# Feed-forward by seven block products: input sums kept in DRAM, other buffer homes, another order in one chunk

## The chip, the cores and the metric

One Trainium2 chip; the kernel runs on one of its cores. The metric is the device time of one execution in microseconds (us). Engines: PE (TensorE) does the matrix products, DVE (VectorE), ACT (ScalarE) and POOL (GpSimd) work elementwise, SP (SyncE) and ACT start the DMA transfers.

## What is computed

One decoder layer on x of 2048 tokens by 1024 channels, in float32:

```python
h = _rmsnorm(x, norm_mix_pre[i])
proj = jnp.einsum("btd,de->bte", h, w_in[i])
...                       # gated short convolution beside a Mamba-2 scan
mix = jnp.einsum("bte,ed->btd", jnp.concatenate([y_a, y_s], axis=-1), w_out[i])
x = x + _rmsnorm(mix, norm_mix_post[i])
h = _rmsnorm(x, norm_mlp_pre[i])
f = jnp.square(jax.nn.relu(jnp.einsum("btd,df->btf", h, w_up[i])))
f = jnp.einsum("btf,fd->btd", f, w_down[i])
x = x + _rmsnorm(f, norm_mlp_post[i])
```

w_up is 1024 x 4096, w_down 4096 x 1024.

## The kernel before

**Mixer.** Four blocks (b) of 512 tokens run one after the other: projections (L154 to L156), convolutions, the scan, the output projection (`out_half`, L166 to L168). What is left of block b at its end (the output projection of group 1, `post_norm`, `mlp_input`) goes into the list `pend` and is emitted by `drain(n)` calls between the stages of block b+1; `mlp_input` writes the normed hidden state, transposed, to `h2_d[b]` in DRAM. After the last block `drain(2)` emits the two halves of its last output projection before the feed-forward part; the other eight entries come by `drain(1)` after each of the first up steps.

**Every product in three.** A float32 operand is split into hi and lo parts (`split`: ACT casts, L609; DVE subtracts, L610), and each product is three matmuls: hi·hi, hi·lo, lo·hi.

**Feed-forward, up.** Two groups g of 1024 tokens. Both matrices are cut 2 x 2 and multiplied with seven block products in place of eight (Winograd's form of Strassen), in the order ORDER = 0, 1, 5, 6, 4, 2, 3. For each group `hidden_blocks` loads 16 tiles of `h2_d` (ring `xt`, 4 tiles), ACT multiplies each by its gain (L657), POOL forms the four sums t1 to t4 per k (L635, L636, L638, L642, ring `us`), and the 28 blocks (7 products x 4 k) are split into 56 tiles that stay for the whole group, k by k: all seven blocks of k = 0, then of k = 1, and so on. Where block i lives is `HOMES[i]`: rings of the mixer used a second time, among them `yh` and `yl`, which hold the inputs of the last output projection. Then for p = 0 to 15: `up_weights(p)` loads four tiles, makes four sums on POOL (L619 to L625) and seven splits into the rings `wh`, `wl` (8 tiles each); `up` does 7 products of 12 matmuls (L690 to L692), 84 per p; DVE adds them up (L697), ACT applies relu and square and its queue stores the result to `f_d`.

**Down weights.** After up(g, p), where p % 2 == g, `down_weights(p)` loads four tiles of w_down, makes four sums, seven splits through the same rings `wh` and `wl`, and stores the 14 parts to `dn_d[p]` from the ACT queue (L682): 18 transfers of 256 KB.

**Down.** For each group eight chunks of two p. `f_load` loads 4 tiles per p (L731, ring `raw`, 6 tiles), makes sums and splits them into the homes; `down_load` loads 14 parts of `dn_d` per p into the homes (L721, L722). A chunk is 28 accumulations (7 products x 4 token tiles) of 6 matmuls (L746 to L748) each. In the first chunk ACT copies them to `acc` tiles (L751), later DVE adds to those (L753). Chunks run product by product; the last chunk of each group is sorted by token tile (`todo.sort`), so that after the seven products of a token tile `combine` and `finish` (norm, gain, residual, store; L759 to L777) can begin.

**Order.** The calls above give instructions; the build lays out each engine's order from what is ready, and places and releases the tiles, so calls of different stages interleave: the first POOL sum of `hidden_blocks(0)` (L635) runs at 1092.4 us, some 400 us before the first up product. A ring tile (`big(tag)`) can be taken again once everything that reads it is done. All tiles here are 128 x 512 float32, 256 KB.

Of the kernel before, what the change touches and what calls it, by code (L numbers as in the profile page):

```python
# [8 lines left out]
F32 = mybir.dt.float32  # L9
F32R = mybir.dt.float32r  # L10
AF = mybir.ActivationFunctionType
ALU = mybir.AluOpType
# [3 lines left out]
P = 128  # L16
T = 2048
D = 1024
KT = D // P
TB = 512  # L20
NB = T // TB
# [4 lines left out]
FF = 4096  # L26
# [3 lines left out]
C_GPRE, C_GMLP, C_GOUT, C_CA, C_CS, C_CB, C_DSK = 0, 8, 16, 32, 56, 104, 116  # L30
# [2 lines left out]
C_ALL = 1536  # L33
BUFS = {
# [4 lines left out]
    "mix": 8, "epx": 2, "eph": 3, "gain": 2,  # L39
    "us": 4, "uc": 8, "acc": 28, "fx": 2,  # L40
}


# [1 line left out]
def hybrid_layer(ctx: ExitStack, tc: tile.TileContext, x, xT, w_in, w_dt, w_out, w_up, w_down,  # L45
# [8 lines left out]
    def big(tag, dt=F32):  # L54
        return sb.tile([P, 512], dt, tag=tag, name=tag, bufs=BUFS.get(tag, 1))
# [403 lines left out]
    def mlp_input(m, tok):  # L459
        for i in range(2):  # L460
            pt = bank()
            for k in range(4):
# [4 lines left out]
            S.dma_start(h2_d[tok // TT][:, i * 4:(i + 1) * 4, t * P:(t + 1) * P],  # L467
                        ht.rearrange("p (k t) -> p k t", k=4))

    gpost = [big("gain") for _ in range(2)]  # L470
    for i in range(2):
        SY.dma_start(gpost[i], rows[0:1, i * 512:(i + 1) * 512].broadcast_to([P, 512]))
# [2 lines left out]
    def drain(n):  # L475
        for _ in range(min(n, len(pend))):
            pend.pop(0)()
# [18 lines left out]
    for b in range(NB):  # L496
# [78 lines left out]
        for h in range(2):  # L575
# [1 line left out]
        ea = [lambda mix=mix, b=b, t=t: post_norm(mix[t], b * TT + t) for t in range(TT)]  # L577
        eb = [lambda mix=mix, b=b, t=t: mlp_input(mix[t], b * TT + t) for t in range(TT)]
        pend += [ea[0], ea[1], eb[0], ea[2], eb[1], ea[3], eb[2], eb[3]]
    drain(2)  # L580

    PB = 2 * TB
    NP = FF // P // 2
    NG = T // PB
    B7 = range(7)
    f_d = [[[dram.tile([P, TB], F32, name=f"f{g}_{f}_{q}") for q in range(2)]
            for f in range(FF // P)] for g in range(NG)]
    dn_d = [[[dram.tile([P, 512], F32, name=f"dn{p}_{i}_{s}") for s in range(2)]  # L590
             for i in B7] for p in range(NP)]

    gmlp = [big("gain") for _ in range(2)]
    for i in range(2):
        S.dma_start(gmlp[i], rows[1:2, i * 512:(i + 1) * 512].broadcast_to([P, 512]))


    HOMES = (("hh",) * 8, ("hl",) * 8, ("xs",) * 6 + ("conv",) * 2, ("xdt",) * 4 + ("z",) * 4,
             ("row",) * 4 + ("m",) * 4, ("yh",) * 8, ("yl",) * 8)

    def home(i, n):
        return HOMES[i][2 * n], HOMES[i][2 * n + 1]

    def ring(i):
        return "wh", "wl"

    def split(v, tags):
        hi, lo = (big(t, F32R) for t in tags)
        S.copy(hi, v)  # L609
        V.tensor_sub(lo, v, hi.bitcast(F32))  # L610
        return hi, lo


    def left(a11, a12, a21, a22, tags, eng):
        out = [None] * 7
        out[0] = split(a11, tags(0))
        out[1] = split(a12, tags(1))
        s1, s2, s3, s4 = (big("us") for _ in range(4))
        eng.tensor_tensor(s1, a21, a22, op=ALU.add)  # L619
        eng.tensor_tensor(s2, s1, a11, op=ALU.subtract)  # L620
        out[5] = split(s2, tags(5))
        eng.tensor_tensor(s3, a11, a21, op=ALU.subtract)
        out[6] = split(s3, tags(6))
        out[4] = split(s1, tags(4))
        eng.tensor_tensor(s4, a12, s2, op=ALU.subtract)  # L625
        out[2] = split(s4, tags(2))
        out[3] = split(a22, tags(3))
        return out

    def right(b11, b12, b21, b22, tags, eng):  # L630
        out = [None] * 7
        out[0] = split(b11, tags(0))
        out[1] = split(b21, tags(1))
        t1, t2, t3, t4 = (big("us") for _ in range(4))
        eng.tensor_tensor(t1, b12, b11, op=ALU.subtract)  # L635
        eng.tensor_tensor(t2, b22, t1, op=ALU.subtract)  # L636
        out[5] = split(t2, tags(5))
        eng.tensor_tensor(t3, b22, b12, op=ALU.subtract)  # L638
        out[6] = split(t3, tags(6))
        out[4] = split(t1, tags(4))  # L640
        out[2] = split(b22, tags(2))
        eng.tensor_tensor(t4, b21, t2, op=ALU.subtract)  # L642
        out[3] = split(t4, tags(3))
        return out

    ORDER = (0, 1, 5, 6, 4, 2, 3)

    def hidden_blocks(g):
        cols7 = [[None] * 4 for _ in B7]
        for k in range(4):  # L650
            raw = {}
            for j in range(2):
                gk = cp[:, C_GMLP + 4 * j + k:C_GMLP + 4 * j + k + 1]
                for q in range(2):
                    raw[j, q] = big("xt")
                    SY.dma_start(raw[j, q], h2_d[2 * g + q][:, 4 * j + k, :])
                    S.activation(raw[j, q], raw[j, q], AF.Copy, scale=gk)  # L657
            blocks = right(raw[0, 0], raw[0, 1], raw[1, 0], raw[1, 1], lambda i: home(i, k), G)
            for i in B7:
                cols7[i][k] = blocks[i]  # L660
        return cols7

    def up_weights(p):
        raw = {}
# [7 lines left out]
    def down_weights(p):  # L672
        raw = {}
        for j in range(2):
            for k in range(2):
                raw[j, k] = big("raw")
                SY.dma_start(raw[j, k].rearrange("p (a b) -> p a b", a=1),
                             w_down[2 * p + j][:, k:k + 1, :])
        blocks = right(raw[0, 0], raw[0, 1], raw[1, 0], raw[1, 1], ring, G)
        for i in ORDER:  # L680
            for s in range(2):
                S.dma_start(dn_d[p][i][s], blocks[i][s].bitcast(F32))  # L682

    def up(g, p, hb7, wb7):
        def product(i):
# [48 lines left out]
    def down(ps_, g, acc, last):  # L734
        first = ps_[0] == 0
        fb = [f_load(g, p, m) for m, p in enumerate(ps_)]
        wb = [down_load(p, m) for m, p in enumerate(ps_)]
        todo = [(i, t) for i in ORDER for t in range(TT)]
        if last:
            todo.sort(key=lambda it: it[1])  # L740
        for n, (i, t) in enumerate(todo):
            ts = slice(t * P, (t + 1) * P)
            pt = bank(("ax", "mm")[n % 2])
            for m in range(len(ps_)):
                (fh, fl), (wh, wl) = fb[m][i], wb[m][i]
                PE.matmul(pt, lhsT=fh[:, ts], rhs=wh, start=(m == 0), stop=False)  # L746
                PE.matmul(pt, lhsT=fh[:, ts], rhs=wl, start=False, stop=False)  # L747
                PE.matmul(pt, lhsT=fl[:, ts], rhs=wh, start=False, stop=(m == len(ps_) - 1))  # L748
            if first:
                acc[i, t] = big("acc")  # L750
                S.copy(acc[i, t], pt)  # L751
            else:
                V.tensor_tensor(acc[i, t], acc[i, t], pt, op=ALU.add)  # L753
            if last and i == ORDER[-1]:
                combine(g, acc, t)
# [14 lines left out]
    def finish(m, tok):  # L770
        r = norm_scale(m, "fx")
        for i in range(2):
# [3 lines left out]
            V.scalar_tensor_tensor(m[i], m[i], r, xt, op0=ALU.mult, op1=ALU.add)  # L776
            S.dma_start(out[tok * P:(tok + 1) * P, i * 512:(i + 1) * 512], m[i])  # L777

    for g in range(NG):
        hb7 = hidden_blocks(g)  # L780
        for p in range(NP):
            wb7 = up_weights(p)
            up(g, p, hb7, wb7)
            drain(1)
            if p % 2 == g:
                down_weights(p)
    for g in range(NG):
        acc = {}
        for p in range(0, NP, 2):
# [42 lines left out]
```

## Time and profile before

| | us |
|---|---|
| three runs | 2862.94, 2860.70, 2855.56; median 2860.7 |
| profiled execution, its time | 2856.19 |
| its span, first to last instruction | 2854.5 |
| mean granted clock of PE in it | 0.980 |

How to read it: the page gives the busy time of each engine and 40 slices; a table of windows gives, for each stretch of time, each engine's busy time with its number of instructions in brackets, the granted PE clock, the share of the DMA engines and their GB/s. Matmuls are pipelined, so PE's busy time hides slow ones; the number of matmuls in a stretch tells more. A list of waits has, for each pair of waiter and releaser, the total in us, the number of times and the longest. A timeline row has start, duration, engine, line, operation, and in brackets the idle time before it and what ended that. A group row has the number of instructions, their busy time in us, and the mean in ns.

### The profile page before, as it was taken

Reading aid. Unit: us, or ns where it says so; the run is one execution under the profiler, and the core shown is the slowest. Engines: PE = TensorE matmul, PEld = TensorE weight load, DVE = VectorE, ACT = ScalarE, POOL = GpSimd, SP = SyncE. Lnnn points to the kernel's source line nnn. Section 1 sums busy time; section 2 is a strip of 40 time slices with the busy share of each in tenths; the row PEclk is TensorE's granted clock in tenths of the full one; section 3 lists DMA queues with packets and bytes.
Section 4 is the critical chain, followed back from the end, with each engine's and each line's share of the span. In section 5 each row is a group of like instructions: output and inputs, shape, how many; then the busy total and the mean of one; then the engine's idle time right before and its main releaser. Section 6 shows DMA issues by size and latency. Waiting matters only on the chain. (4 is left out here: it accounts for less than half of the span.)

```text
span 2854.5 us, 38273 instructions
## 1 busy us (share of the span) xinstructions
PE 2729.4 (96%) x12822; PEld 2240.8 (79%) x12822; DVE 2063.6 (72%) x3511; ACT 1375.0 (48%) x2411; POOL 944.2 (33%) x682
## 2 busy tenths in 40 slices
PE   8999999999999999999998999889999999779995
PEld 6888888888888888888876778678887888668884
DVE  6674966758776677766697667787775777867778
ACT  6445545464454644555565655655555222242221
POOL 1121312213121133211155444464443333553324
PEclk9999999999999999999999999999999999989998
DMA  8323334333343323443326677556668877587774
GB/s 284 121 78 120 104 126 144 121 106 106 121 142 126 108 96 124 139 147 112 103 93 217 229 250 254 192 195 235 233 240 285 283 255 266 195 292 240 244 241 140
DMA packets 290292, 507.20 MB, mean 178 GB/s; under 512 B 31152, under 2 KB 47920, under 8 KB 290096
## 3 DMA queue, kind: packets, MB, share of 16 engines
q1 hardware_dynamic: 213008, 386.77, 41.1%
q10 hardware_dynamic: 77088, 117.99, 11.4%
q8 instruction: 101, 1.65, 0.2%
q14 instruction: 95, 0.78, 0.1%
HBM read 387.07 MB, written 117.57 MB: 177 GB/s over the span
## 5 line engine op out<-in xcount | busy, mean ns | idle before, releaser
L154 PE MATMUL mm<-hh,wh 128*128 128x512 f32 x1408 | 554.8, 394 | 2.2 <-ACT hh L143 2.2
L155 PE MATMUL mm<-hl,wh 128*128 128x512 f32 x1408 | 550.3, 391 | 0.5 <-DVE hl L144 0.5
L156 PE MATMUL mm<-hh,wl 128*128 128x512 f32 x1408 | 550.1, 391 | 0.0
L99 DVE TENSOR_TENSOR wl<-raw,wh 128x512 fp32r<-128x512 f32 x480 | 361.8, 765 | 239.5 <-ACT wh L98 217.8
L98 ACT CAST wh<-raw 128x512 fp32r<-128x512 f32 x480 | 293.8, 618 | 435.6 <-PE mm L155 299.9
L154 PEld LDWEIGHTS mm<-hh,wh 128*128 128x128 f32 x1408 | 265.4, 189 | 57.0 <-ACT hh L143 2.5
L156 PEld LDWEIGHTS mm<-hh,wl 128*128 128x128 f32 x1408 | 265.0, 188 | 55.6
L155 PEld LDWEIGHTS mm<-hl,wh 128*128 128x128 f32 x1408 | 265.2, 188 | 54.7 <-DVE hl L144 1.2
L619 POOL TENSOR_TENSOR us<-raw 128x512 f32<-128x512 f32 x64 | 90.6, 1416 | 465.9 <-DMA raw<-w_up_dram 125.6
L610 DVE TENSOR_TENSOR wl<-us,wh 128x512 fp32r<-128x512 f32 x192 | 202.0, 1077 | 33.6 <-ACT wh L609 23.6
L697 DVE TENSOR_TENSOR uc<-uc,mm 128x512 f32<-128x512 f32 x224 | 150.1, 681 | 74.3 <-PE mm L692 60.2
L166 PE MATMUL ax<-wh,yh 128*128 128x512 f32 x512 | 201.3, 393 | 1.6 <-DVE cst L109 1.6
L168 PE MATMUL ax<-wh,yl 128*128 128x512 f32 x512 | 199.5, 390 | 0.0
L167 PE MATMUL ax<-wl,yh 128*128 128x512 f32 x512 | 199.3, 389 | 0.0
L753 DVE TENSOR_TENSOR acc<-acc,ax 128x512 f32<-128x512 f32 x196 | 133.5, 681 | 56.9 <-PE ax L748 56.8
L219 POOL TENSOR_TENSOR sq<-sq,v 128x512 f32<-128x512 f32 x28 | 37.1, 1326 | 365.2 <-ACT v L218 362.5
L610 DVE TENSOR_TENSOR wl<-raw,wh 128x512 fp32r<-128x512 f32 x144 | 119.2, 840 | 50.5 <-ACT wh L609 33.9
L110 POOL TENSOR_TENSOR cst<-cst 128x1 f32<-128x1 f32 (+1 forms) x76 | 59.2, 779 | 283.8 <-DVE cst L109 283.8
L369 POOL TENSOR_TENSOR row<-row,cT 128x512 f32<-128x512 f32 x60 | 104.4, 1761 | 142.5 <-ACT cT L295 81.1
L753 DVE TENSOR_TENSOR acc<-acc,mm 128x512 f32<-128x512 f32 x196 | 133.2, 680 | 23.1 <-PE mm L748 22.8
L609 ACT CAST wh<-us 128x512 fp32r<-128x512 f32 x192 | 113.2, 616 | 66.9 <-PE mm L691 19.3
L701 ACT ACTIVATE uc<-uc 128x512 f32<-128x512 f32 x128 | 80.7, 631 | 133.1 <-DVE uc L697 129.9
(362 smaller groups left out, 6598.2 us busy)
## 6 DMA issues: line engine op xcount, KB each, us to landing
raw<-w_in_dram SPq DMA_DIRECT2D x352, 256.0 KB, 2.8
raw<-w_out_dram SPq DMA_DIRECT2D x128, 256.0 KB, 2.7
raw<-w_up_dram SPq DMA_DIRECT2D x128, 256.0 KB, 3.6
f<-uc ACTq DMA_DIRECT2D x128, 256.0 KB, 3.5
raw<-f SPq DMA_DIRECT2D x128, 256.0 KB, 4.4
dn<-wh ACTq DMA_DIRECT2D x112, 256.0 KB, 3.3
dn<-wl ACTq DMA_DIRECT2D x112, 256.0 KB, 3.1
row<-cs SPq DMA_DIRECT2D x64, 256.0 KB, 3.8
```

The costliest lines, as they stand in the source:

```text
L98: S.copy(hi, raw)
L99: V.tensor_sub(lo, raw, hi.bitcast(F32))
L154: PE.matmul(pt, lhsT=wh[:, ks], rhs=ah[k], start=(k == 0), stop=False)
L155: PE.matmul(pt, lhsT=wh[:, ks], rhs=al[k], start=False, stop=False)
L156: PE.matmul(pt, lhsT=wl[:, ks], rhs=ah[k], start=False, stop=(k == KT - 1))
L166: PE.matmul(pts[t], lhsT=a, rhs=wh, start=(i == 0), stop=False)
L167: PE.matmul(pts[t], lhsT=a, rhs=wl, start=False, stop=False)
L168: PE.matmul(pts[t], lhsT=c, rhs=wh, start=False, stop=(i == n - 1))
L609: S.copy(hi, v)
L610: V.tensor_sub(lo, v, hi.bitcast(F32))
L697: V.tensor_tensor(c, a, pt, op=ALU.add)
L753: V.tensor_tensor(acc[i, t], acc[i, t], pt, op=ALU.add)
```

## The change

- Input sums: `hidden_sums(g, k)` (four calls per group) loads four tiles of `h2_d`, applies the gain, forms the four sums and stores the seven blocks to `hs_d` from the ACT queue. The calls for group 0 join `pend` after block 2, those for group 1 after block 3. `hidden_blocks` only loads the 28 blocks and splits them, product by product in ORDER instead of k by k. Ring `xt` has 6 tiles instead of 4.
- The `drain(2)` after the last mixer block is gone: all of `pend` comes by one `drain(1)` per p.
- Homes: `HOMES` is now listed in ORDER and uses the rings in the order in which the mixer gives them back; `yh` and `yl` are no homes any more.
- `down_weights` runs at p = 3, 4, 6, 7, 9, 10, 12, 13 of both groups, makes its four sums first (`right_sums`), splits in ORDER, and stores from the SP queue.
- The sort by token tile applies to the last chunk of the last group alone; the last chunk of group 0 stays product by product.
- Rings: `wh`, `wl` 8 to 9, `acc` 28 to 30, `uc` 8 to 7.

```diff
-    "dtk": 1, "raw": 6, "wh": 8, "wl": 8, "hh": 8, "hl": 8, "xt": 4, "xtok": 2,
+    "dtk": 1, "raw": 6, "wh": 9, "wl": 9, "hh": 8, "hl": 8, "xt": 6, "xtok": 2,
...
-    "us": 4, "uc": 8, "acc": 28, "fx": 2,
+    "us": 4, "uc": 7, "acc": 30, "fx": 2,
...
+    hs_d = [[[dram.tile([P, TB], F32, name=f"hs{g}_{i}_{k}") for k in range(4)]
+             for i in B7] for g in range(NG)]
...
-    HOMES = (("hh",) * 8, ("hl",) * 8, ("xs",) * 6 + ("conv",) * 2, ("xdt",) * 4 + ("z",) * 4,
-             ("row",) * 4 + ("m",) * 4, ("yh",) * 8, ("yl",) * 8)
+    HOMES = (("hh",) * 8, ("hl",) * 8, ("row",) * 4 + ("m",) * 4,
+             ("bk", "bk", "bT", "cT", "scm", "xd", "xdh", "xdl"),
+             ("xdt",) * 4 + ("conv",) * 2 + ("carry",) * 2, ("xs",) * 6 + ("u", "v"),
+             ("z",) * 4 + ("xtok", "xtok", "dts", "wdt"))
...
     def home(i, n):
-        return HOMES[i][2 * n], HOMES[i][2 * n + 1]
+        tags = HOMES[ORDER.index(i)]
+        return tags[2 * n], tags[2 * n + 1]
...
+    def right_sums(b11, b12, b21, b22, eng):
+        t1, t2, t3, t4 = (big("us") for _ in range(4))
+        eng.tensor_tensor(t1, b12, b11, op=ALU.subtract)
+        eng.tensor_tensor(t2, b22, t1, op=ALU.subtract)
+        eng.tensor_tensor(t3, b22, b12, op=ALU.subtract)
+        eng.tensor_tensor(t4, b21, t2, op=ALU.subtract)
+        return b11, b21, b22, t4, t1, t2, t3
+
+    def hidden_sums(g, k):
+        raw = {}
+        for j in range(2):
+            gk = cp[:, C_GMLP + 4 * j + k:C_GMLP + 4 * j + k + 1]
+            for q in range(2):
+                raw[j, q] = big("xt")
+                SY.dma_start(raw[j, q], h2_d[2 * g + q][:, 4 * j + k, :])
+                S.activation(raw[j, q], raw[j, q], AF.Copy, scale=gk)
+        blocks = right_sums(raw[0, 0], raw[0, 1], raw[1, 0], raw[1, 1], G)
+        for i in ORDER:
+            S.dma_start(hs_d[g][i][k], blocks[i])
+
+    def hidden_blocks(g):
+        out = [[None] * 4 for _ in B7]
+        for i in ORDER:
+            for k in range(4):
+                raw = big("xt")
+                SY.dma_start(raw, hs_d[g][i][k])
+                out[i][k] = split(raw, home(i, k))
+        return out
...
-    drain(2)
...
+        if b >= NB - 2:
+            pend += [lambda g=b - NB + 2, k=k: hidden_sums(g, k) for k in range(4)]
...
-        blocks = right(raw[0, 0], raw[0, 1], raw[1, 0], raw[1, 1], ring, G)
+        blocks = right_sums(raw[0, 0], raw[0, 1], raw[1, 0], raw[1, 1], G)
         for i in ORDER:
+            halves = split(blocks[i], ring(i))
             for s in range(2):
-                S.dma_start(dn_d[p][i][s], blocks[i][s].bitcast(F32))
+                SY.dma_start(dn_d[p][i][s], halves[s].bitcast(F32))
...
-        if last:
+        if last and g == NG - 1:
             todo.sort(key=lambda it: it[1])
...
+    ahead = list(range(NP))
     for g in range(NG):
...
-            if p % 2 == g:
-                down_weights(p)
+            if 2 < p < NP - 2 and p % 3 != 2:
+                down_weights(ahead.pop(0))
```

More of the change, by code (lines that the diff above doesn't have):

```diff
@@ L468, in mlp_input @@
                         ht.rearrange("p (k t) -> p k t", k=4))
+    PB = 2 * TB
+    NP = FF // P // 2
+    NG = T // PB
+    B7 = range(7)
+    ORDER = (0, 1, 5, 6, 4, 2, 3)
+    f_d = [[[dram.tile([P, TB], F32, name=f"f{g}_{f}_{q}") for q in range(2)]
+            for f in range(FF // P)] for g in range(NG)]
+    dn_d = [[[dram.tile([P, 512], F32, name=f"dn{p}_{i}_{s}") for s in range(2)]
+             for i in B7] for p in range(NP)]
+    hs_d = [[[dram.tile([P, TB], F32, name=f"hs{g}_{i}_{k}") for k in range(4)]
+             for i in B7] for g in range(NG)]
@@ new lines, in hybrid_layer, with home, ring, split @@
+    HOMES = (("hh",) * 8, ("hl",) * 8, ("row",) * 4 + ("m",) * 4,
+             ("bk", "bk", "bT", "cT", "scm", "xd", "xdh", "xdl"),
+             ("xdt",) * 4 + ("conv",) * 2 + ("carry",) * 2, ("xs",) * 6 + ("u", "v"),
+             ("z",) * 4 + ("xtok", "xtok", "dts", "wdt"))
+    def home(i, n):
+        tags = HOMES[ORDER.index(i)]
+        return tags[2 * n], tags[2 * n + 1]
+    def ring(i):
+        return "wh", "wl"
+    def split(v, tags):
+        hi, lo = (big(t, F32R) for t in tags)
+        S.copy(hi, v)
+        V.tensor_sub(lo, v, hi.bitcast(F32))
+        return hi, lo
@@ new lines, in left @@
+    def left(a11, a12, a21, a22, tags, eng):
+        out = [None] * 7
+        out[0] = split(a11, tags(0))
+        out[1] = split(a12, tags(1))
+        s1, s2, s3, s4 = (big("us") for _ in range(4))
+        eng.tensor_tensor(s1, a21, a22, op=ALU.add)
+        eng.tensor_tensor(s2, s1, a11, op=ALU.subtract)
+        out[5] = split(s2, tags(5))
+        eng.tensor_tensor(s3, a11, a21, op=ALU.subtract)
+        out[6] = split(s3, tags(6))
+        out[4] = split(s1, tags(4))
+        eng.tensor_tensor(s4, a12, s2, op=ALU.subtract)
+        out[2] = split(s4, tags(2))
+        out[3] = split(a22, tags(3))
+        return out
@@ L470, in hybrid_layer @@
+    def hidden_blocks(g):
[5 more added lines that the diff above has]
+                out[i][k] = split(raw, home(i, k))
+        return out
     gpost = [big("gain") for _ in range(2)]
@@ L579, in hybrid_layer @@
         pend += [ea[0], ea[1], eb[0], ea[2], eb[1], ea[3], eb[2], eb[3]]
-    drain(2)
[L584 to L591, printed above, removed]
+        if b >= NB - 2:
+            pend += [lambda g=b - NB + 2, k=k: hidden_sums(g, k) for k in range(4)]
     gmlp = [big("gain") for _ in range(2)]
@@ L595, in hybrid_layer @@
         S.dma_start(gmlp[i], rows[1:2, i * 512:(i + 1) * 512].broadcast_to([P, 512]))
-    HOMES = (("hh",) * 8, ("hl",) * 8, ("xs",) * 6 + ("conv",) * 2, ("xdt",) * 4 + ("z",) * 4,
-             ("row",) * 4 + ("m",) * 4, ("yh",) * 8, ("yl",) * 8)
-    def home(i, n):
-        return HOMES[i][2 * n], HOMES[i][2 * n + 1]
[L604 to L611, printed above, removed]
@@ L614, in left @@
[L614 to L628, printed above, removed]
@@ L630, in right @@
[L630 to L661, printed above, removed]
```

## The prediction

> **What bounds the kernel now.** I read the page, then the table of windows over the stages that I found in the 40 slices, then PE's waits, then the timeline where the waits lie. PE is the bound, and the granted clock dips only where it stalls.
>
> ```profile
> span 2854.5 us, 38273 instructions
> PE 2729.4 (96%) x12822; PEld 2240.8 (79%) x12822; DVE 2063.6 (72%) x3511; ACT 1375.0 (48%) x2411; POOL 944.2 (33%) x682
> ...
> PEclk9999999999999999999999999999999999989998
> ```
>
> The 96% hide slow matmuls, so I count matmuls by stage. Each row: length, then each engine's busy time with its instructions, granted clock, DMA share, GB/s.
>
> ```profile
> 1090.00:1440.00 350.00, 349.03 (x1750) 287.92 (x1749) 243.98 (x507) 186.13 (x311) 72.74 (x56) 1.00 0.37 120
> 1496.00:1840.00 344.00, 323.13 (x1390) 260.38 (x1388) 243.49 (x320) 203.56 (x375) 166.36 (x117) 0.98 0.68 231
> 1840.00:1866.00 26.00, 8.62 (x15) 4.06 (x16) 22.88 (x23) 18.67 (x33) 18.16 (x12) 0.60 0.27 91
> 1866.00:2166.00 300.00, 300.00 (x1318) 248.19 (x1318) 229.31 (x282) 177.90 (x311) 148.81 (x97) 1.00 0.68 232
> 2166.00:2184.00 18.00, 10.96 (x34) 8.05 (x33) 9.49 (x10) 5.92 (x11) 6.23 (x4) 0.72 0.86 310
> 2184.00:2474.00 290.00, 289.47 (x1277) 239.39 (x1276) 207.16 (x300) 74.51 (x140) 102.81 (x71) 1.00 0.75 261
> 2474.00:2530.00 56.00, 25.67 (x87) 19.41 (x88) 47.76 (x65) 18.14 (x42) 35.00 (x25) 0.70 0.73 253
> 2530.00:2823.00 293.00, 293.00 (x1294) 242.63 (x1293) 221.09 (x316) 72.65 (x136) 98.28 (x69) 1.00 0.71 242
> 2823.00:2855.00 32.00, 0.45 (x2) 0.02 (x1) 25.55 (x35) 5.05 (x14) 15.81 (x13) 0.58 0.22 82
> ```
>
> The row from 2530 has no stall: 293 / 1294 = 0.2264 us per matmul, so 84 of them (an up p) take 19.0 us and a down chunk of 168 takes 38.0. A window's loss is its length less 0.2264 times its matmuls:
>
> - A, up of group 0 (1496 to 1840): 344 − 314.7 = 29.3
> - B, switch to up of group 1 (1840 to 1866): 26 − 3.4 = 22.6
> - up of group 1: 300 − 298.4 = 1.6
> - C, switch to down (2166 to 2184): 18 − 7.7 = 10.3; the rest of group 0's down: 0.9
> - D, switch from group 0 to 1 in down (2474 to 2530): 56 − 19.7 = 36.3
>
> Together 101.0 us. The last 32 us, without matmuls, are the end of group 1, which stays sorted by token tile; I count no change there. Who ended the stalls:
>
> ```profile
> PE ax L746 <- DMA hh<-dn: 33.6, 3, 22.7
> PE mm L690 <- ACT wh L609: 13.6, 5, 7.0
> PE mm L690 <- ACT hh L609: 9.2, 2, 6.3
> PE mm L692 <- DVE wl L610: 9.1, 8, 2.2
> ...
> PE mm L690 <- DVE uc L697: 1.6, 1, 1.6
> ```
>
> The first is C and D (loads of down weights into homes), the third B (hidden blocks), the others A and B (weight splits).
>
> **D: group 0's last chunk product by product.** Sorted by token tile, the chunk reads every home until its last token tile, so group 1's first loads can't start before; hence the 22.7 us. In product order a home is free after its four accumulations (4 x 6 x 0.2264 = 5.4 us), as between all other chunks, which lose 0.9 us together. That wait goes. What is late next: `combine` and `finish` of all four token tiles now become ready together, at the chunk's end, while group 1's first chunk needs 28 new acc tiles and 30 are there.
>
> ```profile
> L776 DVE SCALAR_TENSOR_TENSOR acc<-acc,cst,fx 128x512 f32<-128x512 f32 x15 | 20.3, 1393 | 5.3 <-DMA fx<-x 4.4 <-POOL cst L110 0.9
> L773 DVE TENSOR_TENSOR acc<-acc,gain 128x512 f32<-128x512 f32 x8 | 5.4, 678 | 0.0
> L763 DVE TENSOR_TENSOR acc<-acc 128x512 f32<-128x512 f32 x4 | 5.4, 1340 | 4.0 <-POOL acc L762 4.0
> L764 DVE TENSOR_TENSOR acc<-acc 128x512 f32<-128x512 f32 x4 | 4.5, 1114 | 0.0
> L761 DVE TENSOR_TENSOR acc<-acc 128x512 f32<-128x512 f32 x4 | 3.1, 773 | 0.0
> L760 DVE TENSOR_TENSOR acc<-acc 128x512 f32<-128x512 f32 x4 | 2.9, 725 | 0.0
> ```
>
> DVE needs 16 x 1.393 + 8 x 0.678 + 5.4 + 4.5 + 3.1 + 2.9 = 43.6 us for this, some 46 with the small norm steps (estimate), and 14 splits for the next chunk at about 0.9 (estimate between 0.678 and the 1.145 below), 12.6: 59 us against the 38.0 of a chunk whose accumulations ACT copies. Excess 21. PE can run ahead by 8 PSUM banks and 2 spare acc tiles, 10 x 6 x 0.2264 = 13.6. I take a loss of 10 (bounds 0 and 25: all hidden; the excess and a cold restart in full). D gains 26.
>
> **B: hidden blocks made ahead.** Before, k = 0 holds the four `us` sums until the homes of its last products are free, that is until group 0's last product; only then come loads, gains, sums and splits of k = 1 to 3. After, product 0's four tiles can be split 6 x 2.72 = 16.3 us before the switch (12 matmuls, 2.72 us per product), six tiles being loaded ahead; then a product's homes become free each 2.72 us and are wanted 19.0 us later. POOL's 16 sums and ACT's 16 gains leave this place. Added: 28 loads for 16. Prices:
>
> ```profile
> L610 DVE TENSOR_TENSOR wl<-us,wh 128x512 fp32r<-128x512 f32 x95 | 106.6, 1145 | 8.7 <-ACT wh L609 8.6
> L697 DVE TENSOR_TENSOR uc<-uc,mm 128x512 f32<-128x512 f32 x110 | 73.7, 682 | 41.8 <-PE mm L692 41.5
> L657 ACT ACTIVATE xt<-xt,cst 128x512 f32<-128x512 f32 x32 | 22.5, 718 | 17.6 <-DMA xt<-h 17.5
> L638 POOL TENSOR_TENSOR us<-xt 128x512 f32<-128x512 f32 x8 | 13.0, 1622 | 0.0
> 2180.00:2190.00 10.00, 9.92 (x44) 7.83 (x43) 0.69 (x1) 4.20 (x8) 0.00 (x0) 1.00 1.02 376
> ```
>
> In the 16.3 + 19.0 = 35.3 us around the switch DVE does 28 + 7 splits and 14 adds: 35 x 0.678 (a two-input DVE step without POOL beside it, as in L773 above) + 14 x 0.682 = 33.3 us, or 49.6 at 1.145. Bytes: 28 + 8 loads and 8 stores of 0.262 MB, 11.5 MB, 31 us at the 376 GB/s of the last row. Both just fit. I take 6 of the 22.6 (bounds 0 and 17), near the cheap end, because POOL has 4 sums there and not 16 more. B gains 16.6.
>
> One rule is weighed here. In the windows the clock is 0.60 in B and 0.70 in D, so part of a loss is slow matmuls and not waiting. The Trainium skill ("TensorE: Matmul & The Clock Gate", What's actually happening) says that PE drops to half clock after an idle window of about 3.4 us and needs as long of work to return. The trace agrees: after B's waits of up to 7.0 us the clock is 0.60, and the row from 1866 with no such wait has 1.00. By that rule three short waits in B would cost 4 us and not 6, and the sum below would be 2 us less.
>
> **A: start of up, group 0.** Removed here: 16 POOL sums per group in front of the first products (16 x 1.622 = 26 us of POOL, each slowing DVE, 1.145 against 0.678); the wait of two products for `yh` and `yl`; `down_weights` at p = 0 and 2, whose parts kept `wh`/`wl` until stored. Added: 96 matmuls of block 3's output projection (21.7 us, moved here from before 1496, no gain in itself) that can fill PE while hidden tiles are split. Moved: block 3's `post_norm` two p later; group 1's sums at p = 10 to 13. I take 14 of 29.3 (bounds 5 and 34): the stalls near 1500 to 1530 and half of the later small ones go. A gains 15.3.
>
> **C.** SP's order delayed the loads:
>
> ```profile
> 2138.03 22.02 SPq L731 DMA_DIRECT2D raw<-f  x7
> 2167.31 0.42 SPq L721 DMA_DIRECT2D hh<-dn  x1
> ```
>
> Seven `raw<-f` loads held SP for 22 us because `raw` was full, partly with `down_weights(15)`; the first `hh<-dn` went out at 2167.31, after the stage's end. The change makes no down weights after p = 13, so 18 transfers and four `raw` tiles are out of the way; the wait of `raw` for the last homes stays. I take 5 of 10.3 (bounds 0 and 10). C gains 5.3.
>
> **What it costs elsewhere.** `down_weights` twice in three p: DVE has 14 splits and 7 adds there, 14 x 1.0 (estimate between 0.678 and 1.145) + 7 x 0.682 = 18.8 us of 19.0, followed by a p with 11.8. Group 1's up: 5 in place of 1.6 (bounds 1 and 12). In the mixer, 16 loads, 28 stores, 16 gains (11.5 us of ACT) and 16 sums (26 us of POOL) join block 3, where the row from 1090 has DVE busy 244 of 350 us, ACT 186, POOL 73, DMA 0.37. That covers it; without the cover it would be the sums' 26. I take 3 (bounds −3, from the larger rings, and 20). ACT's queue loses 224 stores of down parts to SP (SP's side is rival 3) and gets 56 of hidden blocks; in p = 10 to 13 up's stores to `f_d` stand behind those that wait for POOL sums, and behind them ACT's casts and relus: at worst a sum's 1.6 us each, hidden by ACT's 48%. One `uc` tile fewer costs nothing while DVE keeps up with PE, and PE waited for its adds 1.6 us in all.
>
> **Sum.** Losses after: 14 + 6 + 5 + 5 + 0.9 + 10 + 3 = 43.9 against 101.0, a gain of 57 us. The profiled execution took 2856.2 (span 2854.5 and 1.7 around it), 4.5 under the median of the three runs, 2860.7; 2856.2 − 57 = 2799.
>
> **The rivals.**
>
> 1. *The acc tiles take the place of the homes (0.13).* DVE runs `finish` before group 1's splits, PE waits for acc copies and then for splits: D keeps 25. For: DVE's 59 against 38. Against: 10 accumulations of slack. Such a DVE jam at B as well (11 more) gives 2799 + 15 + 11 = 2825.
> 2. *DMA in group 0, p = 10 to 13 (0.09).* With both down weights and hidden sums a p moves 8 + 18 + 11 = 37 tiles, 9.7 MB, 25.8 us at 376 GB/s against 19.0: p = 10 falls 6.8 behind, p = 11 gives back 5.8, p = 12 and 13 add 6.8 each, a backlog of 14.6 us, behind which come the 28 hidden loads. For: 231 GB/s already. Against: the stores have no one waiting but the rings. 15 in A and 7 in B: 2821.
> 3. *Slower: stores at the head of SP's queue (0.08).* SP, which had only loads, now waits in turn for each of 224 parts to be split, and the next `w_up` loads are queued behind that; PE waits for their splits. In the trace of before SP waits for such releases up to 7.7 us:
>
> ```profile
> SPq L677 <- DVE wl L610: 10.3, 3, 7.7
> ```
>
> 16 times 7.7 beyond what ring `raw` hides is 123 us: 2799 + 123 = 2922. It decides from 57 / 16 = 3.6 us per `down_weights` on. Against: loads run up to a p ahead (19 us).
> 4. *The mixer pays (0.05).* A POOL sum holds up DVE, as 1.145 against 0.678 shows; if PE waited for all 16 in block 3, 26 in place of 3: 2822. The Trainium skill ("SBUF — State Buffer", Who interferes with whom) calls the ports shared by DVE and GpSimd an exclusive lock; that speaks for this price, and 244 of 350 us against its reaching PE.
> 5. *Nothing gained (0.05).* DVE at 72% is the true limit, and each stall removed comes back later: 2856.
>
> **How the numbers follow.** Forecast 0.56 (2780 to 2818). Better than that, nearly all gone at the low bounds, 0.04: 2856 − 97 = 2759. Rivals 1, 2 and 4, still faster: 0.27. About 0.3%, 9 us, can be told from no change. Faster 0.56 + 0.04 + 0.13 + 0.09 + 0.05 = 0.87, less 0.01 for what ends within 0.3%: 0.86; same 0.06; slower 0.08. The range leaves out rivals 3 and 5 (0.13) and the extreme of the better case: 2768 (88 gained) to 2840 (rivals 1 or 2 with the dearer up of group 1 and mixer).
>
> **What would show it.** Right: no wait of over 10 us for `hh<-dn`, and the stretch between the groups in down at a clock near 1.00; POOL's hidden sums before the end of the mixer; PE's matmul count per us across the first switch near 1 / 0.2264. D wrong: PE's waits name ACT's `acc` copies or DVE's adds. C and SP wrong: SP's waits for L610 grow, and PE waits for `wh`. B wrong: PE waits for L609 or L610 of hidden tiles, or `xt<-hs` landings. I am wrong as a whole if PE's 0.2264 us per matmul itself changes, or block 3 lengthens by over 20 us.

## The result and the profile after

The changed kernel takes 2825.4 us, the median of four runs (2819.99 to 2828.29), against 2860.29 for the kernel before (2855.56 to 2862.94): ratio 0.9878, 95% interval 0.9858 to 0.9898. The sign and the range of the prediction held. The size did not: 35 us were gained, by the medians, where 57 were forecast. One execution of a later kernel took 4582.04 us at a granted clock of 0.557, against 2793.8 to 2802.34 us of its other three, and is left out.

The page of the kernel after, first lines and the clock in 40 slices:

```profile
span 2822.9 us, 38911 instructions
PE 2725.5 (97%) x12822; PEld 2241.2 (79%) x12822; DVE 2086.8 (74%) x3511; ACT 1364.8 (48%) x2409; POOL 939.0 (33%) x682
...
PEclk9999999999999999999999999899999999999997
```

The same 12822 matmuls, and the shares of the engines hardly moved. The profiled execution took 2824.66 us, 31.5 less than that of before. Where the 31.5 came from is read as the prediction did it: a stretch's loss is its length less 0.2264 us for each matmul in it. The cuts are the first matmul of a step or chunk, so the stretches differ a little from the round ones of the prediction. First before: the three parts of stage A (p = 0 to 2 with what is left of the output projection ahead of them, p = 3 to 8, p = 9 to 15), the first step of group 1 (B), and the four chunks around the switch in down (D):

```profile
1448.70:1572.50 123.80, 109.56 (x478) 88.24 (x476) 99.36 (x132) 70.61 (x134) 67.88 (x50) 0.96 0.49 164
1572.50:1700.80 128.30, 121.68 (x521) 97.95 (x522) 87.86 (x114) 76.83 (x143) 60.58 (x43) 0.97 0.70 238
1700.80:1836.90 136.10, 134.71 (x589) 109.92 (x588) 97.77 (x127) 82.53 (x145) 64.48 (x44) 1.00 0.71 240
1836.90:1880.50 43.60, 26.04 (x86) 17.94 (x86) 39.53 (x41) 26.87 (x47) 30.59 (x20) 0.73 0.34 115
...
2443.40:2632.90 189.50, 158.64 (x674) 129.20 (x673) 141.69 (x197) 57.89 (x117) 86.78 (x61) 0.91 0.71 243
```

Then the windows of the kernel after: the same three, the first step of group 1, the rest of group 1's up, chunks 0 to 6 of group 0's down, and the four chunks around the switch in down.

```profile
1456.20:1560.80 104.60, 102.96 (x463) 85.18 (x462) 76.86 (x113) 55.66 (x102) 41.84 (x29) 1.00 0.46 151
1560.80:1701.00 140.20, 126.48 (x537) 100.74 (x536) 93.11 (x133) 83.49 (x161) 66.32 (x52) 0.94 0.76 261
1701.00:1867.20 166.20, 142.93 (x590) 114.23 (x589) 115.24 (x130) 93.36 (x167) 95.72 (x62) 0.92 0.84 296
1867.20:1887.10 19.90, 19.30 (x86) 15.66 (x85) 19.90 (x33) 16.28 (x31) 3.95 (x2) 1.00 0.77 274
1887.10:2172.70 285.60, 285.60 (x1261) 236.54 (x1260) 229.84 (x282) 173.42 (x307) 144.87 (x95) 1.00 0.74 259
2172.70:2439.30 266.60, 266.60 (x1178) 220.79 (x1177) 199.88 (x266) 73.03 (x129) 86.06 (x60) 1.00 0.79 262
2439.30:2601.40 162.10, 155.53 (x674) 126.86 (x673) 145.65 (x197) 55.91 (x117) 85.70 (x61) 0.99 0.83 286
```

For example, 1701.0 to 1867.2 is 166.2 us long and has 590 matmuls, 133.6 us at the full rate: 32.6 are lost, and the clock of 0.92 stands in the same row. All stretches, in us:

| stretch | before | forecast | after |
|---|---|---|---|
| mixer, later start of the last output projection | 0 | 3 | 7.5 |
| A, up of group 0 | 28.7 | 14 | 51.0 |
| of it p = 0 to 2 / 3 to 8 / 9 to 15 | 15.6 / 10.3 / 2.8 | | −0.2 / 18.6 / 32.6 |
| B, switch (first step of group 1) | 24.1 | 6 | 0.4 |
| rest of group 1's up | −0.1 | 5 | −0.1 |
| C, switch to down, with group 1's last step | 6.9 | 5 | −0.2 |
| group 0's chunks 0 to 6 | 3.7 | 0.9 | −0.1 |
| D, four chunks around the switch in down | 36.9 | 10 | 9.5 |
| sum | 100.2 | 43.9 | 68.0 |

The rows of this table are worked out from windows as above; the mixer's is 1456.2 − 1448.7, the first matmul of that last projection in both. (The prediction's stretch C reached into chunk 0: its 10.3 us are spread over the rows C and chunks 0 to 6 here.) The sums differ by 32.2 us, and the last matmul comes 31.5 us earlier (2823.06 and 2791.54). So B, C, D and the chunks between gave 62 us, and half of that was lost again: 22.3 in A and 7.5 in the mixer. The list of PE's waits of the kernel after says what A waits for:

```profile
PE mm L695 <- ACT wh L498: 21.6, 10, 7.5
PE mm L697 <- DVE wl L499: 12.3, 9, 4.4
...
PE ax L463 <- ACT mix L457: 4.7, 2, 3.7
...
PE mm L751 <- DVE acc L758: 2.5, 1, 2.5
```

L498 and L499 are the splits (L609, L610 before). The loads `hh<-dn`, which stood first with 33.6 us, are gone from the list; `wh` and `wl`, the split weights, have taken the head. One such wait, in the timeline of the kernel after:

```profile
1750.76 1.26 POOL L508 TENSOR_TENSOR us<-raw 128x512 f32<-128x512 f32 x1 [19.51 <-DMA raw<-w_up_dram]
...
1753.39 0.62 ACT L498 CAST wh<-us 128x512 fp32r<-128x512 f32 x1 [2.31 <-POOL us L509]
...
1754.07 0.79 PE L695 MATMUL mm<-row,wh 128*128 128x512 f32 x1 [7.49 <-ACT wh L498]
```

Read upwards: PE stood for 7.49 us until ACT had cast `wh`, ACT waited for a POOL sum, and POOL had been idle for 19.51 us until an up weight landed. The weights come too late; neither ACT nor POOL is short of time there. What makes them late is the question of the experiments.

### The profile page after: what moved, and what is told of

Read it like the earlier page. It is cut to its first block, busy times and chain, and to the rows that moved or that the text cites. A ratio compares the mean times of both kernels' runs of the same rounds, so it can differ in the third digit from the quotient of the medians.

```text
span 2822.9 us, 38911 instructions
## 1 busy us (share of the span) xinstructions
PE 2725.5 (97%) x12822; PEld 2241.2 (79%) x12822; DVE 2086.8 (74%) x3511; ACT 1364.8 (48%) x2409; POOL 939.0 (33%) x682
## 5 line engine op out<-in xcount | busy, mean ns | idle before, releaser
L99 DVE TENSOR_TENSOR wl<-raw,wh 128x512 fp32r<-128x512 f32 x480 | 368.1, 778 | 236.2 <-ACT wh L98 225.8
L499 DVE TENSOR_TENSOR wl<-us,wh 128x512 fp32r<-128x512 f32 x192 | 188.4, 999 | 73.8 <-ACT wh L498 59.2
L499 DVE TENSOR_TENSOR wl<-raw,wh 128x512 fp32r<-128x512 f32 x144 | 138.1, 966 | 38.6 <-ACT wh L498 24.9
L498 ACT CAST wh<-us 128x512 fp32r<-128x512 f32 x192 | 113.4, 616 | 56.9 <-POOL us L509 29.9
```

Source lines behind the costliest of these rows:

```text
L99: V.tensor_sub(lo, raw, hi.bitcast(F32))
```

## The experiments

Losses below are those of the table, by the same count. The expectations count a step from its first matmul to the next step's, less 19.02 us; that includes the PE transposes of block 3's `post_norm` (L463), so by it p = 3 to 8 of the kernel after loses 26.1 and not 18.6; in p = 9 to 15 the two counts are 33.1 and 32.6. In kernels that do not touch them, p = 0 to 2 came out between −0.2 and 4.4, D between 9.5 and 16.1, and p = 3 to 8 between 11.1 and 21.6, so differences of some 5 us in the first two, and of up to 10 in p = 3 to 8, are scatter. Medians are compared with 2825.4; each ratio is to the kernel before, on the same chip.

The theory was that p = 9 to 15 stall because the transfers of two things meet there: four steps' down weights (p = 9, 10, 12 and 13, where before there were three, p = 10, 12 and 14) and group 1's input sums (p = 10 to 13). Against it stood POOL's sums, the order on SP's queue, and the ring that up and down weights share.

### Group 1's sums left out

```diff
-                SY.dma_start(raw, hs_d[g][i][k])
+                SY.dma_start(raw, hs_d[0][i][k])
...
-        if b >= NB - 2:
-            pend += [lambda g=b - NB + 2, k=k: hidden_sums(g, k) for k in range(4)]
+        if b == NB - 2:
+            pend += [lambda g=0, k=k: hidden_sums(g, k) for k in range(4)]
```

Group 1 works on group 0's blocks: its 16 loads, 16 gains, 16 sums and 28 stores are left out of the computation.

> Leaves out hidden_sums for group 1 (group 1's up reads the blocks of group 0). In the changed kernel the seven up steps p = 9 to 15 of group 0 take 166 us from first matmul to first matmul where 133 would be without a stall, 33 lost. If the sums of group 1 are the cause, by bytes, by SP's order or by POOL, the 33 fall to under 8 and the time to about 2795. If the two-in-three down weights alone are (their parts on SP's queue), at least 20 of the 33 stay and the time is about 2815.

2799.21 us, ratio 0.9797 (0.9782 to 0.9812). Its window for p = 9 to 15:

```profile
1707.30:1840.60 133.30, 133.30 (x590) 110.40 (x589) 106.10 (x128) 81.56 (x147) 68.02 (x47) 1.00 0.76 263
```

The loss there is gone (133.3 against 133.6), with all four down weights still in place; p = 3 to 8 keeps 21.6. So group 1's sums are needed for the stall. The next two ask which part of them.

### Group 1's POOL sums left out

```diff
+        if g:
+            blocks = (raw[0, 0], raw[1, 0], raw[1, 1], raw[1, 0], raw[0, 1], raw[1, 1], raw[0, 1])
+        else:
+            blocks = right_sums(raw[0, 0], raw[0, 1], raw[1, 0], raw[1, 1], G)
```

All loads, gains and stores stay; the seven blocks of group 1 are plain tiles, so its sums are left out of the computation.

> Group 1's sums keep all their loads, gains and seven stores per k, but store loaded blocks in place of the POOL sums (group 1's result is that of other blocks). Bytes theory and SP theory: the loss in steps p = 9 to 15 stays at 25 or more, time 2820 to 2826. POOL theory (16 sums of 1.6 us and the ring of four sum tiles hold up the weight sums): it falls by 15 or more, time about 2808.

2815.24 us, ratio 0.985 (0.9836 to 0.9865).

```profile
1697.20:1859.90 162.70, 142.03 (x590) 113.32 (x589) 108.06 (x131) 92.66 (x166) 69.05 (x45) 0.94 0.85 298
```

POOL's busy time fell from 95.72 us to 69.05, and 29.1 of 32.6 us of loss stayed. POOL is not the cause; its sums are worth some 3 us here. The time fell by 10 us, below the 2820 to 2826 expected with a staying loss; 7.5 of it lie in p = 3 to 8 (11.1 lost), where the edit changes nothing.

### Twelve of 28 stored blocks fewer per group

Three of the seven blocks of each k are plain tiles of `h2_d`. Here only the four others are stored, and `hidden_blocks` loads the plain ones from `h2_d` and applies the gain.

```diff
-        for i in ORDER:
+        for i in (5, 6, 4, 3):
             S.dma_start(hs_d[g][i][k], blocks[i])
```

> Only the four true sums per k go through DRAM; the three blocks that are parts of the input are loaded from the hidden state again and get their gain again (12 more ACT steps of 0.72 us per group where the blocks are split). 12 stores fewer per group, 3 of 11 tiles per step. Bytes theory: 37 tiles become 34, the loss of 33 in p = 9 to 15 falls by 7 to 15; the switch to group 1 may lose up to 8 by ACT's gains: time about 2817. Order theory: three of seven loads no longer wait for a store of the sums, the loss falls by half or more: about 2808.

2815.41 us, ratio 0.9851 (0.9836 to 0.9867). The loss in p = 9 to 15 falls to 18.3, and the switch, where gains stand again in front of the splits, loses 4.1 in place of 0.4.

```profile
1701.80:1853.40 151.60, 140.93 (x589) 114.08 (x588) 109.22 (x135) 96.08 (x174) 88.39 (x60) 0.95 0.87 303
```

303 GB/s for 151.6 us are 45.9 MB; the kernel after moves 296 x 166.2 = 49.2 MB in these steps. With 3.3 MB less the loss is 14 us less.

### Down weights of p = 10, 12 and 13 done in group 1 instead

```diff
-            if 2 < p < NP - 2 and p % 3 != 2:
+            if p in ((3, 4, 6, 7, 9), (1, 2, 3, 4, 6, 7, 8, 10, 11, 12, 13))[g]:
```

> down_weights in group 0 only at p = 3, 4, 6, 7, 9, in group 1 at eleven of p = 1 to 13; all else as changed. A p with sums then moves 19 tiles and not 37. Bytes theory: the 33 lost in p = 9 to 15 fall under 10; group 1 with more down weights stays under 8 (27 tiles fit a step at 376 GB/s, 26 are moved): time about 2805. Order theory (SP at loads that wait for the sums' stores): at least 15 of the 33 stay, time 2815 or more.

2795.6 us (2793.24 to 2797.85), ratio 0.9782 (0.9766 to 0.9797): 30 us below the kernel after, and with the next kernel the fastest here. Its p = 9 to 15, and the rest of group 1's up:

```profile
1701.90:1835.20 133.30, 133.30 (x589) 110.36 (x588) 89.31 (x111) 80.95 (x145) 71.51 (x51) 1.00 0.79 268
...
1855.30:2123.70 268.40, 267.22 (x1177) 220.48 (x1176) 243.11 (x276) 168.32 (x302) 158.65 (x102) 1.00 0.86 305
```

The loss of p = 9 to 15 is gone once more, now with group 1's sums in place. Group 1 takes three down weights more, at 305 GB/s, for 1.9 us. So neither the three late down weights nor the sums stall p = 9 to 15 alone; both together do.

### The early ones moved too

```diff
-            if 2 < p < NP - 2 and p % 3 != 2:
+            if p in ((0, 1, 2, 9), (1, 2, 3, 4, 5, 6, 8, 9, 10, 11, 12, 13))[g]:
```

> down_weights in group 0 only at p = 0, 1, 2 and 9, in group 1 at twelve of p = 1 to 13. The losses of 26 at p = 3 to 8 (beside the last block's post_norm) and of 33 at p = 9 to 15 should go if both come from down weights beside other loads and stores; p = 0 to 2, with the 96 matmuls of the output projection, take 3 steps of parts at a cost under 8, group 1 under 5: time about 2780. If the loss at p = 3 to 8 is post_norm alone, about 2800.

2801.4 us, the median of three (2793.8 to 2802.34), ratio 0.9792 (0.9775 to 0.9809). By the time alone this is what the expectation named for block 3's `post_norm` as the cause (about 2800). Where the loss lies needs a profile, and the one taken was of the execution of 4582.04 us; so the kernel was run again:

> The same kernel as in the run before it: down weights after p = 0, 1, 2 and 9 of group 0 and after twelve steps of group 1, none after p = 3 to 8. What is asked is the loss of p = 3 to 8 (six up steps of 19.0 us at full rate), 26 us with the change as it stands and 25 with the down weights of p >= 10 moved to group 1. Theory 1 (transfers and splits of the down weights beside what is left of block 3 make that loss): p = 3 to 8 loses under 8 us, p = 0 to 2 and group 1 together get at most 10 dearer, and the time stays near 2797, since the last steps of a group cost little anyway. Rival (block 3's post norm and its transfers on the shared engines make it by themselves): p = 3 to 8 still loses 18 to 26, and what the time then gains or loses comes from other steps. Either way p = 9 to 15 loses under 5, as where both down weights of p >= 10 were taken out, and D loses 9 to 14.

2797.55 us (2791.99 to 2798.3), ratio 0.9782 (0.9766 to 0.9798). Windows of p = 0 to 2, p = 3 to 8, the first step of group 1 and the rest of its up:

```profile
1456.80:1572.00 115.20, 104.90 (x463) 84.51 (x461) 86.61 (x127) 62.52 (x114) 48.99 (x33) 1.00 0.68 230
1572.00:1694.90 122.90, 119.94 (x529) 98.24 (x529) 87.05 (x115) 74.94 (x142) 59.93 (x44) 0.97 0.52 176
...
1829.20:1854.40 25.20, 21.04 (x85) 15.36 (x84) 23.67 (x36) 20.46 (x38) 6.14 (x4) 1.00 0.78 258
1854.40:2124.90 270.50, 268.90 (x1178) 221.70 (x1177) 244.50 (x282) 172.52 (x310) 162.37 (x106) 0.99 0.90 319
```

p = 3 to 8 now loses 3.1 (8.8 by the count of the expectation, just over its bound of 8 and far from the rival's 18). It is also far under the 11.1 to 21.6 of the kernels that leave these steps alone. So what is left of block 3 does not make that loss alone; it takes the down weights too. But p = 0 to 2 pays 10.4, the first step of group 1 6.0 and the rest 3.8, where the kernel with late down weights pays 3.3, 0.6 and 1.9. Against that kernel it is 14 us more there and 15 us less in p = 3 to 8: moved, not removed. Against the kernel after, p = 0 to 2 and group 1 got 20 us dearer; the expectation of at most 10 missed.

### More bytes in group 1

```diff
+            if g and 9 < p < 14:
+                for n in range(11):
+                    S.dma_start(junk_d[p - 10][n], f_d[g][2 * p - 2 + n % 2][n // 2 % 2])
```

Forty-four copies of 256 KB from DRAM to DRAM are added in group 1, eleven per p, as many transfers as a p of group 1's sums has.

> Adds to group 1's up, which loses nothing in the changed kernel, the bytes that group 1's sums move in group 0: 11 copies of 256 KB between tensors in DRAM per step p = 10 to 13, on ACT's queue, with nothing that waits for them and nothing to wait for. Bytes theory: group 1 then loses about what group 0 loses at p = 10 to 15, 15 to 33, time 2840 to 2858. Order theory (in group 0 it is SP's queue standing at loads that wait for the stores of sums, not the bytes): under 8 lost, time under 2833.

2835.82 us, ratio 0.9924 (0.9906 to 0.9942), between the two forecasts. The window in which 33 of the copies were issued:

```profile
2023.00:2156.00 133.00, 133.00 (x588) 110.16 (x587) 99.16 (x120) 76.41 (x135) 71.22 (x48) 1.00 0.86 310
```

PE lost nothing there at 310 GB/s. The last copies went out at up to 2179 us, beside the loads of the first chunk of group 0's down: of the 10 us that the kernel got slower, 4.4 lie in that group's first chunks, and the rest in places of known scatter. A mean rate of up to 310 GB/s does not by itself stall PE. The stalled stretch of p = 9 to 15 wants more: 49.2 MB in the 133.6 us that its matmuls need are 368 GB/s.

### Each queue and ring by itself

Three kernels keep the transfers and change who waits for them. The stores of down parts back on ACT's queue:

```diff
-                SY.dma_start(dn_d[p][i][s], halves[s].bitcast(F32))
+                S.dma_start(dn_d[p][i][s], halves[s].bitcast(F32))
```

> Down-weight parts are stored from ACT's queue again, as before the change; all else as changed. SP theory (weight loads stand in SP's queue behind parts that wait for their split): the loss in steps p = 9 to 15 halves at least, time about 2805 or less. Bytes theory: the same bytes, no more than 8 us either way, 2818 to 2833. Group 1's up, which loses nothing as changed, should lose nothing here either by the bytes theory; if ACT's casts stand behind the stores it loses some 10.

2866.54 us, ratio 1.0028 (1.0016 to 1.004): 41 us slower than the kernel after, and slower than before. p = 3 to 8, p = 9 to 15 and group 1's up:

```profile
1559.80:1720.20 160.40, 128.51 (x537) 104.77 (x536) 97.93 (x134) 88.06 (x164) 69.94 (x53) 0.88 0.69 234
1720.20:1893.00 172.80, 144.69 (x590) 115.94 (x590) 105.70 (x131) 92.72 (x162) 82.91 (x59) 0.91 0.79 277
...
1912.00:2189.00 277.00, 270.22 (x1178) 221.33 (x1177) 208.91 (x261) 163.13 (x287) 139.08 (x91) 0.99 0.70 245
```

The losses are 38.8, 39.2 and 10.3 against 18.6, 32.6 and −0.1. Neither theory had a time like this; only the last sentence of the expectation, some 10 in group 1 if ACT's casts stand behind the stores, came true. The list of ACT's waits, from p = 3 to the end of group 0's up, names the way:

```profile
ACT wh L498 <- DMA dn<-wh: 30.1, 16, 3.6
```

ACT's next cast into a `wh` tile waits, 16 times, until the store of the part in that tile has landed, and the store stood in ACT's own queue behind other casts and relus. In the kernel after the same list has 5.3 us of it in two waits (for `dn<-wl`).

The loads of hidden tiles and blocks on ACT's queue, so that they stand behind no store of a part:

```diff
-                SY.dma_start(raw[j, q], h2_d[2 * g + q][:, 4 * j + k, :])
+                S.dma_start(raw[j, q], h2_d[2 * g + q][:, 4 * j + k, :])
...
-                SY.dma_start(raw, hs_d[g][i][k])
+                S.dma_start(raw, hs_d[g][i][k])
```

> All loads of hidden state and of its blocks go out from ACT's queue and not SP's, so SP no longer stands in front of weight loads and parts at a load that waits for the sums' stores. Same bytes, same rings. Order theory: of the 33 lost in group 0 at p = 9 to 15 at least 15 go, time about 2808. Ring theory (tiles of the ring raw or of wh and wl are held too long whatever queue the loads are in): at least 25 stay, 2822 or more.

2850.42 us, ratio 0.9972 (0.9959 to 0.9984). That is 25 us slower than the kernel after: p = 9 to 15 loses 37.6, the switch 13.0, p = 0 to 2 9.9. A ring of its own for the down weights:

```diff
+    "rdn": 4, "us": 4, "uc": 7, "acc": 30, "fx": 2,
...
-                raw[j, k] = big("raw")
+                raw[j, k] = big("rdn")
```

> down_weights loads into a ring of its own, 4 tiles, so up's weight loads need not wait for tiles that it holds; queues and bytes as changed. Ring theory: the losses at p = 3 to 8 (26) and p = 9 to 15 (33) fall by 20 or more together, time about 2803. Order theory: SP still stands, at least 45 of the 59 stay, 2815 or more.

2830.4 us, ratio 0.9901 (0.9886 to 0.9915). p = 9 to 15 loses 32.7, as with the shared ring; p = 3 to 8 loses 13.7 in place of 18.6, which is within its scatter. In the kernel after a load of a down weight had held SP's queue once for 18.7 us in these steps; with the own ring none of these waits is over 5.4, and PE gained nothing by it. The stall of p = 9 to 15 outlives each of these edits.

### The order of the splits, and the order of the chunk

Sums made ahead, but loaded and split k by k:

```diff
-        for i in ORDER:
-            for k in range(4):
+        for k in range(4):
+            for i in ORDER:
```

> Hidden blocks made ahead, but loaded and split k by k as before the change, in place of product by product. If the order is what took the stall at the switch to group 1's up away (23 lost before, 1 as changed), at least 10 come back there: time 2835 or more. If the sums made ahead are, under 5 come back: under 2831.

2841.0 us, ratio 0.9937 (0.9921 to 0.9953), 16 us slower than the kernel after. The switch loses 4.7 against 0.4, so with the sums made ahead (and the other homes and the larger ring `xt`, which this kernel keeps) some 20 of B's 24 us are gone whatever the order, and the order adds at most 4. What the order would do alone was not run. The time missed the forecast of under 2831, because the rest of the 16 lies elsewhere: in p = 0 to 2 (6.7 more; group 0's splits change their order too) and D (6.1 more), partly scatter.

Both last chunks sorted by token tile, as before:

```diff
-        if last and g == NG - 1:
+        if last:
```

> Undoes the product-major last chunk of group 0 alone. By the prediction the switch between the groups in down loses 36 again in place of 10: 2825 + 26 = 2851. Rival: the earlier stall was due to the old homes and to 28 acc tiles, and the order matters little: under 2835.

2848.46 us, ratio 0.9962 (0.9949 to 0.9974), 23 us slower than the kernel after. The four chunks around the switch in down, and PE's longest wait:

```profile
2442.60:2628.50 185.90, 155.72 (x674) 127.88 (x673) 145.24 (x197) 57.94 (x116) 82.87 (x61) 0.92 0.74 247
```

```profile
PE ax L751 <- ACT bT L498: 28.4, 1, 28.4
```

185.9 − 0.2264 x 674 = 33.3 us are lost, 23.8 more than in the kernel after. PE waits 28.4 us in one piece before group 1's first product. The list puts it down to a cast into `bT`, which ended just before, but the matmul that waited reads `hh`:

```profile
2505.13 0.42 SPq L726 DMA_DIRECT2D hh<-dn  x1
2509.22 0.77 PE L751 MATMUL ax<-hh 128*128 128x512 f32 x1 [28.38 <-ACT bT L498]
```

Loads of `hh<-dn` took 3.6 to 5.7 us to land in this stretch, so the load of 2505.13 came in at about the time when PE went on. As in the kernel before, then, the wait is most likely one for group 1's first down weights. They went out late: the sorted chunk's last matmul had begun at 2480.46.

## Why the prediction was right, and where it was wrong

**D was right in its size, and its cause only in part.** Forecast 10, measured 9.5, at a clock of 0.99, and the sort alone brings 23.8 back (forecast 26). But homes held by the sorted chunk are not all of the wait: with the sort, the first load of `hh` left 24.7 us after the chunk's last matmul had begun, and SP's list of waits from 2470 to 2510 has 20.0 us that end with output stores (`out_dram<-acc`). How much is homes and how much SP's order was not told apart. What came next was also named: the waits left there are for ACT's and DVE's `acc` (2.5 us the longest), so rival 1 is there in kind, with 9.5 us and not 25.

**B, C and the rest of group 1's up were forecast too dear.** B was to keep 6 and kept 0.4; C 5 and −0.2; group 1's up 5 and −0.1. The prediction had DVE at 18.8 of 19.0 us in a p with down weights, and `raw` waiting for homes; in the row from 1887.1 DVE is busy 229.84 of 285.60 us and PE all of them. B falls mostly with the sums made ahead; the order on top of that is worth at most 4.

**A is the step that failed.** "I take 14 of 29.3 (bounds 5 and 34): the stalls near 1500 to 1530 and half of the later small ones go." Its first half held: p = 0 to 2 fell from 15.6 to −0.2. The second had the wrong sign: the later stalls grew from 13.1 to 51.2, and A's 51.0 lies above its upper bound of 34. The prediction counted for them only what leaves (sums, `yh` and `yl`, the down weights of p = 0 and 2). What arrives (the same eight down weights of the group now within p = 3 to 13, and group 1's sums) it costed on DVE, and on the DMA engines only in rival 2, with a chance of 0.09.

**Rival 2 named the place and the two things that meet; its price was too low.** It expected p = 10 to 13 to fall behind by 14.6 us at 376 GB/s, 15 in A and 7 in B. Measured were 32.6 in p = 9 to 15 and nothing at B. That both must meet is shown: without group 1's sums, or without the late down weights, the loss is 0; with 3.3 MB less it is 18.3; POOL, the ring and the queues changed alone leave 29 to 39. That the DMA engines' rate sets the size of the loss is not shown. Over the whole stretch the rate was 277 to 303 GB/s in all kernels, but that is a mean of full and idle parts. In the kernel after, PE's waits of over 1 us all end between 1740 and 1828; three windows there, and one at D:

```profile
1737.00:1759.00 22.00, 13.21 (x45) 9.43 (x45) 10.66 (x14) 11.28 (x21) 8.08 (x6) 0.78 0.98 336
1759.00:1777.00 18.00, 18.00 (x79) 14.82 (x79) 16.17 (x16) 9.61 (x17) 17.69 (x12) 0.98 0.39 145
1777.00:1828.00 51.00, 36.52 (x144) 27.87 (x143) 29.75 (x37) 25.02 (x45) 24.93 (x18) 0.87 0.92 329
2520.00:2560.00 40.00, 36.38 (x160) 29.50 (x159) 36.80 (x55) 15.48 (x30) 18.17 (x13) 1.00 1.03 384
```

In the first, with PE's longest wait, the DMA engines are full (0.98). In the second PE loses nothing, SP's queue stands for 18.7 us at one load of a down weight, and the engines fall to 0.39. Had they stayed full at the first row's 336 / 0.98 = 343 GB/s, the 49.2 MB would take 143 us, 10 more than the matmuls need, and none at the last row's rate (an estimate). So the bytes alone account for 0 to 10 of the 32.6; the rest comes from elsewhere, such as waits that leave the engines idle, as in the second row.

In p = 3 to 8 the loss is 18.6 with down weights beside block 3's leftovers and 3.1 without; the leftovers themselves were not taken out. These steps move 36.6 MB (261 GB/s for 140.2 us) for 121.6 us of matmuls: 301 GB/s, less than the 310 at which group 1 lost nothing. The mean rate does not explain this loss.

**What stays open.** How much of the stall in p = 9 to 15 is full DMA engines, and how much is loads and stores that wait for each other through rings and queues when so many meet, was not told apart. No kernel took the late splits away and left their transfers, so a part of DVE and ACT in it is not excluded. Why the kernel with early and late down weights moved pays at the switch has not been followed either.

**Rival 3 had the right waits and the wrong sign for the total.** SP does wait for splits at the stores of parts, by the list of SP's waits of the kernel after:

```profile
SPq L687 <- ACT wh L498: 91.7, 53, 7.5
...
SPq L687 <- DVE wl L499: 35.8, 51, 3.6
```

127.5 us of it, close to the 123 that the rival feared. But group 1, with eight down weights, loses nothing beside them, and taking the stores off SP costs 41 us. PE does wait for `wh`, which the prediction named as the sign that SP is at fault, and the trace shows its way at work ahead of the wait of 7.49 us:

```profile
1725.87 0.38 SPq L672 DMA_DIRECT2D raw<-w_up_dram  x1
...
1742.40 0.53 SPq L672 DMA_DIRECT2D raw<-w_up_dram  x1
```

For 16.5 us SP sent no up weight; between the two it sent 12 stores of parts and one hidden load. From 1726 to 1752 it waited 6.3 us for the casts of parts, and 2.5 us at up weights themselves. So SP's order has a share in this wait. Its size in the whole stall is not known, because the kernel that took the stores off SP put a larger wait on ACT. ACT's relief of 224 stores was given no value at all, and its undoing costs more than that of any other part tried: without it the change would have made nothing faster (ratio 1.0028).

**The mixer** paid 7.5 instead of 3, far from rival 4's 26. **Rival 5** is out: DVE's share rose from 72% to 74% and the time fell; in the late-weights kernel it fell further.

By size the miss is: A 37 us dearer and the mixer 4.5, B, C, group 1's up, D and the chunks 17.4 cheaper; together 24 of the 57 forecast. That the range held owes something to luck: 2825 is outside the 2780 to 2818 of the forecast proper and at the prices of rivals 1 and 2 (2825 and 2821), and without the 17.4 of misses the other way the time would have been some 2842, past the range's end of 2840.

## What to carry to other kernels

When work is moved to where an engine has time, add up the bytes of the stage it goes to, over the time that the stage takes without a stall, and compare the rate with what long busy stretches of the same kernel sustain (here 260 to 319 GB/s), not with the best 10 us. Here this warns of p = 9 to 15 (368), but not of p = 3 to 8 (301), where the order of the waits has to be read. A store belongs on a queue whose engine is not itself the one that needs the stored tile back: here the same 224 stores cost 41 us more on ACT than on SP, although SP waited 127 us for them. Two pieces of background work that each hide alone should be given different steps: moving three of eight down weights out of the steps with the input sums gained 30 us.

## What the runs showed of the hardware

The rate of a short stretch was no guide to that of a long one: 376 GB/s over 10 us before, about half of it on ACT's queue, which only stores there (DMA share 1.02); 384 over 40 us at D (share 1.03); 336 over the 22 us with PE's longest wait (share 0.98); and 277 to 303 over 150 to 173 us of loads and stores with PE waiting, at a DMA share of 0.79 to 0.87. The Trainium skill ("DMA: Bandwidth & Descriptors", Specifications) has about 358 GB/s as one core's share of the memory; the 10 us and the 40 us are above it, and the highest rate of the long windows here is 319.

The same page (Issuing engines are not separate DMA queues) says that transfers started by different engines run on the same DMA engines, so that spreading them saves only the time of starting them, which is usually small. No saving shows here either: moving the hidden loads from SP to ACT took 25 us more (2850.42 against 2825.4 us). The choice of queue is not small, though: with the stores of parts on ACT in place of SP the same bytes took 41 us more, and there ACT's casts waited 30.1 us, in 16 waits, for tiles that its own queued stores still held.

The granted clock fell with PE's waits, 0.92 in p = 9 to 15 and 0.88 in p = 3 to 8 with the stores on ACT, where waits of up to 13.1 us stand, and was 1.00 where no wait was left. So some of each loss is slow matmuls after a wait, as the prediction weighed for B.
